# State space loop of a hybrid trunk step: one of the four products that turn the states forth goes by a ScalarE copy and Pool, and three inputs are scaled in front of the loop

## The chip, the cores and the metric

The kernel runs on one core of a Trainium2 chip. The metric is device time of one execution in microseconds (us). The engines are TensorE (PE in the rows; PEld is its weight load), VectorE (DVE), ScalarE (ACT), GpSimd (POOL, "Pool" in the text) and SyncE (SP), which issues most of the transfers.

## The reference, cut to what matters

Two layers run over a prompt group of 512 tokens and a sample group of 8 x 4 = 32 tokens with shared weights. Layer 1's token mixer is a diagonal complex state space:

```python
def _s5(u, h0_re, h0_im, a_re, a_im, log_dt, b_re, b_im, c_re, c_im, d_skip, w_glu):
    ...                                                  # ab = discretised pole, bb = discretised input matrix
    def block_step(carry, u_blk):
        h_re, h_im = carry
        bu_re = jnp.einsum('bcgi,gpi->bcgp', u_blk, bb_re)
        bu_im = jnp.einsum('bcgi,gpi->bcgp', u_blk, bb_im)
        bu_re = bu_re.at[:, 0].add(ab_re * h_re - ab_im * h_im)
        bu_im = bu_im.at[:, 0].add(ab_re * h_im + ab_im * h_re)
        ...
        _, _, s_re, s_im = lax.associative_scan(_cplx_affine_combine, (a_r, a_i, bu_re, bu_im), axis=1)
        y = (jnp.einsum('bcgp,gip->bcgi', s_re, c_re)
             - jnp.einsum('bcgp,gip->bcgi', s_im, c_im) + d * u_blk)
        return (s_re[:, -1], s_im[:, -1]), y
    ...
    z = jnp.einsum('bld,de->ble', jax.nn.gelu(y), w_glu)
    out = z[..., :D_MODEL] * jax.nn.sigmoid(z[..., D_MODEL:])
```

Each layer then adds a cross-attention to a memory of 256 rows, whose keys and values are `mem @ w_k` and `mem @ w_v`, and a squared-ReLU MLP.

## The kernel before, in words

Prompt and sample go together: the activations are eight tiles of 128 channels x 544 columns, and in the state space layer the 544 columns are four groups of 136 (8 of the sample, 128 of the prompt). A weight block is used in two parts, high and low: ScalarE copies the high part (helper line L137, tile `whl`), and DVE or Pool subtracts it to get the low part (L177). For the eight memory key blocks of layer 1 it is Pool that subtracts.

The order of the work is written out by hand: `s5_layer` (L1811) appends steps to a list, and `run` calls them one after the other. Every engine executes its instructions in the order in which the steps emit them; the framework adds only the semaphore waits between engines. It adds them for PSUM by bank: two engines that touch the same bank wait for each other, also where the columns differ and where both only read.

The part that matters is the loop over the eight channel tiles, `kt` = 0 to 7. Its order on all engines is: states(0), K0; then for kt = 0 to 6: states(kt+1), from kt = 3 on parts(kt-3), the key block K(kt+1), outs(kt), from kt = 1 on fetch(kt-1). After it come four value blocks (L467), outs(7) and the gated product (L227, L215). In the texts below, E(m), K(m), outs(m) and so on stand for these steps' parts with index m.

- **states(m)** (L1918): TensorE multiplies the inputs into PSUM banks 0 to 3 (L1926, E(m), 16 instructions). ScalarE fills the decay factors `rho`. DVE turns the inputs back by a table `ro` of cosines and sines (L1937 twice, L1938, L1939, L1940, and L1942 for the sample), scans real and imaginary part in banks 4 and 5 (L1944 twice, tiles `ks`), and turns the states forth by four products of 128x512, two of each `ks` with the two halves of `ro` (L1954, L1955, for x = 1, then for x = 0). Pool adds and subtracts the products (L1956 for the outputs' states, L1957 for the last states); ScalarE copies the sample's start states in (`h0v`, two small copies). SP loads the tables of step m+2, and Pool scales the input of step m+2 (`scale`, L1907).
- **K(m)** (L450, 24 matmuls): one block of the memory keys of layer 1, put into bank 7, columns 0 to 255. ScalarE reads it out (`kv_out` L430: a copy of 128x256), and SP stores it.
- **outs(m)** (L1967): TensorE makes the output in four groups q = 0 to 3, each one L1975 and two L1978 (2 and 4 instructions in the trace). Groups 0 to 2 go to bank 6, group 3 to bank 7, columns 256 to 391. ScalarE applies gelu (128x408 and 128x136), and its queue stores the result.
- **parts(m)** (L1995): ScalarE copies the high part of a gelu output (128x544), Pool subtracts for the low part (L2000).

In front of the loop, `begin` (L1887) makes the scale row `ru`; DVE scales the inputs 0 and 1, and Pool sets the first columns of the two `rho` tiles (L1903).

Of the kernel before, what the change touches and what calls it, by code (L numbers as in the profile page):

```python
# [9 lines left out]
AF = mybir.ActivationFunctionType  # L10
# [7 lines left out]
KT = 8  # L18
# [39 lines left out]
class Trunk:  # L58
# [1752 lines left out]
    def s5_layer(self, att_begin, kre):  # L1811
        nc, I, O = self.nc, self.I, self.O
        V = nc.vector
# [6 lines left out]
        def tr(kt):  # L1820

            if kt % 3 == 2:
                return [t[:, :512] for t in D["r2"]]
            return [D["ar"][0][:, 2048 + kt % 3 * 1024 + x * 512 :][:, :512] for x in range(2)]

        def load_e(kt):
            if kt < KT:
                nc.sync.dma_start(te(kt), self.tab[kt][:, 0:1024])

        def load_r(kt):  # L1830
            if kt < KT:
                for x, r in enumerate(tr(kt)):
                    nc.sync.dma_start(r, self.tab[kt][:, 2560 + 512 * x : 3072 + 512 * x])
# [53 lines left out]
        def begin():  # L1887

            y, b0, b1 = self.sm["y"], self.aux[1], self.aux[0][:, 128:256]
            for j in range(4):  # L1890
                nc.tensor.transpose(b0[:, j * 128 : j * 128 + 128], y[:, j : j + 1].to_broadcast([P, 128]), self.ident)
            nc.tensor.transpose(b1, y[:, 4:5].to_broadcast([P, 128]), self.ident)
            D["ru"] = ru = self.rb[:, :TAU]
            for s in range(4):
                a, r = 3 - s, slice(32 * s, 32 * s + 32)
                self.act(ru[r, 8:], b0[r, a * 128 : a * 128 + 128], AF.Copy)
                V.tensor_copy(ru[r, :8].rearrange("p (f j) -> p f j", f=2),
                              b1[r].rearrange("p (j x) -> p j x", x=32)[:, :, a : a + 8 : 4].rearrange("p j f -> p f j"))
            scale(0)
            scale(1)  # L1900
            D["rho"] = [self.slot(), self.slot()]
            for t in D["rho"]:
                nc.gpsimd.memset(q4(t)[:, :, :1], 0.0)  # L1903

        def scale(kt):
            up = D["up"][kt].rearrange("p (q j) -> p q j", q=4)
            (nc.gpsimd if kt > 1 else V).tensor_mul(up, up, D["ru"].unsqueeze(1).to_broadcast([P, 4, TAU]))  # L1907
# [6 lines left out]
        ks = [self.banks[:, 4 + x] for x in range(2)]  # L1914
# [3 lines left out]
        def states(kt):  # L1918
            def fn():
                E = te(kt)  # L1920
                up = D["up"][kt]
                for v in self.mmv:
                    self.touch(self.mm, v)
                for x in range(2):
                    for q in range(4):
                        nc.tensor.matmul(es[:, x, q // 2, q % 2], E[:, x * 512 + q * 128 : x * 512 + q * 128 + 128],  # L1926
                                         up[:, q * TAU : q * TAU + TAU], start=True, stop=True)
                ro = tr(kt)
                ah = D["ah"]
                qs = slice(4 * kt, 4 * kt + 4)  # L1930

                rho = D["rho"][kt % 2]
                self.act(q4(rho)[:, :, 1:], self.rho[:, qs].unsqueeze(2).to_broadcast([P, 4, 127]), AF.Copy)

                m = [self.slot()[:, :512] for _ in range(2)]
                for x in range(2):
                    V.tensor_mul(q22(m[x]), ec[:, x], q22(ro[1]))  # L1937
                V.tensor_mul(ec, ec, q22(ro[0]).unsqueeze(1).to_broadcast([P, 2, 2, 2, 128]))  # L1938
                V.tensor_add(q22(ks[0]), ec[:, 0], q22(m[1]))  # L1939
                V.tensor_sub(q22(ks[1]), ec[:, 1], q22(m[0]))  # L1940
                av = ah[:, :, qs].rearrange("p x (a q) j -> p x a q j", a=2)
                V.tensor_add(av, av, es[:, :, :, :, :8])  # L1942
                for k in ks:
                    V.tensor_tensor_scan(k, rho[:, :512], k, 0.0, ALU.mult, ALU.add)  # L1944
                hh = [self.slot(), self.slot()]
                hv = [t.rearrange("p (q j) -> p q j", q=4) for t in hh]
                for x in range(2):
                    self.act(hv[x][:, :, :8], D["h0v"][:, x, qs], AF.Copy)
                    nc.gpsimd.memset(hv[x][:, :, 8:9], 0.0)
                hp = D["hp"]  # L1950

                for x, op in ((1, ALU.add), (0, ALU.subtract)):
                    p, r = self.slot(), self.slot()
                    V.tensor_mul(p[:, :512], ks[0], ro[x])  # L1954
                    V.tensor_mul(r[:, :512], ks[1], ro[1 - x])  # L1955
                    nc.gpsimd.tensor_tensor(hv[x][:, :, 9:], q4(p)[:, :, :127], q4(r)[:, :, :127], op=op)  # L1956
                    nc.gpsimd.tensor_tensor(hp[x][:, qs], q4(p)[:, :, 127], q4(r)[:, :, 127], op=op)  # L1957
                D["H", kt] = hh
                if kt == 0:
                    D["r2"] = [self.slot(), self.slot()]  # L1960
                load_e(kt + 2)
                load_r(kt + 2)
                if kt + 2 < KT:
                    scale(kt + 2)
            return Step(fn, deep=1)

        def outs(kt):  # L1967
# [83 lines left out]
        def last_kv():  # L2051
# [3 lines left out]

        kv[0][1].deep = -1
        S += [Step(aux_kv), kv[0].popleft(), Step(stats, deep=-1), kv[0].popleft(), Step(self.stat_rsqrt, deep=-1), Step(begin),
              kv[0].popleft(), kv[0].popleft(), Step(free_kv), states(0), kv[1].popleft()]
        for kt in range(KT - 1):
# [161 lines left out]
```

## Time and profile before

| what | value |
|---|---|
| median of 3 runs | 1545.75 us (1545.52 to 1546.58) |
| the profiled execution, its own time | 1544.09 us |
| span of the profiled execution | 1542.3 us |
| mean granted TensorE clock | 0.991 |
| busy share of the span | PE 97%, DVE 66%, ACT 45%, POOL 13% |
| the state space loop | about 833 to 899 us of the span |

The profile is of one execution, which took 1544.09 us by its own time; the span of its instructions is 1542.3 us, and the 1.8 us between them lie around the instructions. Busy shares over the whole span are means over stages with different limits, so the loop is read by itself: by windows of 10 us, by the timeline of each engine, and by the chain of waits.

### The profile page before, as it was taken

To read this page: it belongs to the slowest core of one execution; us is meant where nothing else is said; L and a number is where in the kernel's file an instruction comes from. 1 tells how busy PE (TensorE), PEld (TensorE's weight loads), DVE (VectorE), ACT (ScalarE), POOL (GpSimd) and SP (SyncE) were. 2 spreads that over 40 slices of the span, in tenths; PEclk is the share of its full clock that TensorE was granted. 3 is DMA by queue.
4 is the path that set the end of the run, shared out by engine and by line. 5 is a ranking of instruction groups with operands and counts; after the bars stand their busy time and mean duration, and the time that the engine had idled before them with its cause. 6 is when DMAs were issued, how large, how long until landed. Compare 5 with 4: busy or idle time off the path is not lost.

```text
span 1542.3 us, 29330 instructions
## 1 busy us (share of the span) xinstructions
PE 1494.1 (97%) x11927; PEld 1446.7 (94%) x11927; DVE 1015.5 (66%) x2068; ACT 687.2 (45%) x1278; POOL 200.3 (13%) x167
## 2 busy tenths in 40 slices
PE   8999979999999999999999999999999999999996
PEld 8999869988999999999998889998899999999995
DVE  6896786444577566666756964553479677585864
ACT  6332454343445433665444443343357445272543
POOL 2555550000000000000103760000000000000001
PEclk9999989999999999999999999999999999999998
DMA  7765526363323343333587975336322414141211
GB/s 278 182 153 148 169 85 230 131 242 124 111 80 105 135 134 134 134 134 107 179 268 230 333 242 184 110 137 264 133 69 83 137 55 149 44 139 53 85 53 59
DMA packets 92535, 224.49 MB, mean 146 GB/s; under 512 B 12496, under 2 KB 42976, under 8 KB 88304
## 3 DMA queue, kind: packets, MB, share of 16 engines
q1 hardware_dynamic: 87440, 211.06, 40.3%
q0 software_dynamic: 1792, 6.37, 2.3%
q10 hardware_dynamic: 3168, 5.18, 0.9%
q8 instruction: 94, 1.54, 0.4%
q14 instruction: 41, 0.34, 0.1%
HBM read 192.78 MB, written 29.80 MB: 144 GB/s over the span
## 4 chain that ended last, share of the span: by engine, by line
PE 78%; DVE 8%; ACT 1%; issue 1%; POOL 1%; DMA 0%; SPq 0%; ACTq 0%; DVEq 0%; POOLq 0%
PE banks L215 44%; PE banks L1403 12%; PE banks L1295 10%; PE banks L467 2%; PE banks L956 2%; PE banks L892 2%; PE banks L973 1%; PE banks L876 1%; PE banks L227 1%; PE banks L1382 1%; DVE banks L1944 1%; ACT slot L137 1%; DVE banks L702 1%; PE banks L1766 0%; DVE whl L177 0%
## 5 line engine op out<-in xcount | busy, mean ns | idle before, releaser
L215 PE MATMUL banks<-slot,whl 128*128 128x272 f32 x6264 | 802.1, 289 | 5.8 <-ACT slot L137 2.4
L215 PEld LDWEIGHTS banks<-slot,whl 128*128 128x128 f32 x6264 | 791.1, 188 | 11.0 <-ACT slot L137 4.5
L137 ACT ACTIVATE whl<-wst 128x1024 fp32r<-128x1024 f32 (+1 forms) x236 | 218.7, 930 | 134.8 <-PE banks L1403 47.8
L177 DVE TENSOR_TENSOR whl<-wst,whl 128x1024 fp32r<-128x1024 f32 x137 | 171.1, 1252 | 92.1 <-ACT whl L137 89.4
L137 ACT ACTIVATE slot<-banks 128x512 fp32r<-128x512 f32 (+8 forms) x134 | 61.1, 479 | 144.1 <-PE banks L215 42.2
L1403 PE MATMUL banks<-slot,whl 128*128 128x272 f32 x912 | 120.2, 289 | 0.5 <-DVE rt L1316 0.5
L1403 PEld LDWEIGHTS banks<-slot,whl 128*128 128x128 f32 x912 | 116.7, 188 | 0.7 <-DVE rt L1316 0.7
L1295 PE MATMUL banks<-slot,whl 128*128 128x272 f32 x756 | 97.2, 288 | 0.9 <-DVE tmp L1413 0.9
L1295 PEld LDWEIGHTS banks<-slot,whl 128*128 128x128 f32 x756 | 95.6, 188 | 1.1 <-ACT whl L137 1.1
L1525 POOL TENSOR_TENSOR slot<-slot,slot 128x272 f32<-128x272 f32 x6 | 5.0, 855 | 616.1 <-ACT slot L137 616.1
L137 ACT ACTIVATE slot<-x,vec 128x544 fp32r<-128x544 f32 (+2 forms) x50 | 35.3, 728 | 108.7 <-DVE x L2013 43.8
L1413 DVE TENSOR_TENSOR tmp<-banks,rb 128x544 f32<-128x544 f32 x30 | 21.7, 725 | 83.0 <-PE banks L1403 83.0
L1403 PE MATMUL banks<-slot,arena_mlp 128*128 128x272 f32 x528 | 71.5, 288 | 0.4 <-DVE rt L1316 0.4
L702 DVE SCALAR_TENSOR_TENSOR banks<-slot,vec,banks 128x512 f32<-128x512 f32 x90 | 67.9, 755 | 2.8
L1403 PEld LDWEIGHTS banks<-slot,arena_mlp 128*128 128x128 f32 x528 | 68.2, 188 | 0.6 <-DVE rt L1316 0.6
L1295 PE MATMUL banks<-slot,arena_mlp 128*128 128x272 f32 x504 | 65.3, 288 | 0.4 <-DVE acc L1330 0.4
L1295 PEld LDWEIGHTS banks<-slot,arena_mlp 128*128 128x128 f32 x504 | 63.9, 188 | 0.7 <-DVE acc L1330 0.6
L425 POOL TENSOR_TENSOR slot<-slot,slot 128x512 fp32r<-128x512 f32 x4 | 6.1, 1566 | 371.4 <-ACT slot L137 371.4
L137 ACT ACTIVATE tmp<-x 128x544 f32<-128x544 f32 x40 | 25.9, 647 | 63.4 <-DVE x L1099 39.7
L137 ACT ACTIVATE tmp<-banks 128x544 f32<-128x544 f32 x32 | 19.9, 623 | 76.5 <-PE banks L215 76.5
L177 POOL TENSOR_TENSOR whl<-wst,whl 128x1024 fp32r<-128x1024 f32 x19 | 45.3, 2386 | 57.4 <-ACT whl L137 57.4
L250 DVE TENSOR_TENSOR slot<-tmp,slot 128x544 fp32r<-128x544 f32 x32 | 23.2, 726 | 41.5 <-ACT slot L137 41.5
(280 smaller groups left out, 2063.3 us busy)
## 6 DMA issues: line engine op xcount, KB each, us to landing
wst<-in_w SPq DMA_DIRECT2D x231, 512.0 KB, 4.4
arena_att<-in_kc SPq DMA_DIRECT2D x16, 1024.0 KB, 5.0
arena_att<-in_vc SPq DMA_DIRECT2D x16, 1024.0 KB, 5.3
tab<-arena_prep SPq DMA_DIRECT2D x24, 512.0 KB, 3.8
whl<-in_w POOLq DMA_DIRECT2D x12, 512.0 KB, 6.0
arena_s<-tab SPq DMA_DIRECT2D x8, 768.0 KB, 5.5
arena_s<-tab SPq DMA_DIRECT2D x8, 512.0 KB, 6.3
arena_s<-tab SPq DMA_DIRECT2D x12, 256.0 KB, 5.2
```

Source lines behind the costliest of these rows:

```text
L137: self.nc.scalar.activation(out, in_, func, **kw)
L177: eng.tensor_sub(t[:, 1].bitcast(F32R), src, t[:, 0])
L215: self.nc.tensor.matmul(ps[:, c, :HALF], w, x[:, c * HALF : c * HALF + HALF], start=first and n == 0, stop=last and n == len(seq) - 1)
L227: self.nc.tensor.matmul(ps[:, c, :HALF], self.w8(b, kt)[wi], rhs[kt][xi].bitcast(F32R)[:, c * HALF : c * HALF + HALF], start=first and kt ...
L250: self.nc.vector.tensor_sub(l.bitcast(F32R), src_h if src_l is None else src_l, h)
L467: nc.tensor.matmul(ps[m], self.memt(2 * kp + k2, xi)[:, m * 128 : m * 128 + 128], t[:, wi, k2 * 512 : k2 * 512 + 512], start=kp == 0 and k ...
L702: nc.vector.scalar_tensor_tensor(A, win(k), w(k), A, op0=ALU.mult, op1=ALU.add)
L892: nc.tensor.matmul(o, qs[qi], ks[ki], start=e == 0 and i == 0, stop=e == 1 and i == 2)
L956: nc.tensor.matmul(ps[e], vs[vi], xs[xi], start=m == 0 and i == 0, stop=m == 1 and i == 2)
L1295: nc.tensor.matmul(bank, u[:, wi, k * 128 : k * 128 + 128], x[k][xi].bitcast(F32R), start=n == k == 0, stop=n == 2 and k == 3)
L1403: nc.tensor.matmul(ps[:, c, :HALF], us[kt // 4][:, wi, kt % 4 * 128 : kt % 4 * 128 + 128], M["h"][kt][xi].bitcast(F32R)[:, c * HALF : c * ...
L1413: job("V", 0.7, lambda: V.tensor_mul(self.c2(t), self.psv(ps), self.c2(self.rb)), [*bk, "rb"], [("t", o % 2)])
```

## The change

In `begin`, the inputs 0 to 4 are scaled, and not 0 and 1 alone; `scale` still puts 0 and 1 on DVE and the others on Pool. In the loop, only states(3), (4) and (5) scale an input (5, 6 and 7). In states(m), ScalarE copies `ks[1]` (the scan in bank 5) to a slot `kc`, Pool multiplies that with `ro[1]`, and the subtraction for x = 0 takes this product; DVE keeps three products.

```diff
-            scale(0)
-            scale(1)
+            for kt in range(5):
+                scale(kt)
...
+                kc, r1 = self.slot(), self.slot()
+                self.act(kc[:, :512], ks[1], AF.Copy)
+                nc.gpsimd.tensor_mul(r1[:, :512], kc[:, :512], ro[1])
+
                 for x, op in ((1, ALU.add), (0, ALU.subtract)):
-                    p, r = self.slot(), self.slot()
+                    p, r = self.slot(), r1
                     V.tensor_mul(p[:, :512], ks[0], ro[x])
-                    V.tensor_mul(r[:, :512], ks[1], ro[1 - x])
+                    if x:
+                        r = self.slot()
+                        V.tensor_mul(r[:, :512], ks[1], ro[0])
                     nc.gpsimd.tensor_tensor(hv[x][:, :, 9:], q4(p)[:, :, :127], q4(r)[:, :, :127], op=op)
                     nc.gpsimd.tensor_tensor(hp[x][:, qs], q4(p)[:, :, 127], q4(r)[:, :, 127], op=op)
...
-                if kt + 2 < KT:
+                if 2 < kt < KT - 2:
                     scale(kt + 2)
```

In the changed file the Pool product is L1954, the products on DVE are L1958 and L1961, the sums on Pool L1962 and L1963, and the matmuls of outs L1981 and L1984.

The order of ScalarE around states(1), K1 and outs(0), before and after. `slot_8969` and `slot_8974` take K1 out of bank 7; the 128x408 and 128x136 rows are the gelus of outs(0).

```order
L137 ACTIVATE slot_8789<-rho 128x4x127
L137 ACTIVATE slot_8923<-slot_8472 128x4x8
L137 ACTIVATE slot_8924<-slot_8472 128x4x8
L137 ACTIVATE slot_8969<-banks 128x256 [waits PE_49]
L137 ACT_TABLE_LOAD [waits DVE_49]
L137 ACTIVATE slot_8984<-banks 128x408 [waits PE_49]
L137 ACTIVATE slot_8984<-banks 128x136 [waits PE_49]
```

```order
L137 ACTIVATE slot_8792<-rho 128x4x127
L137 ACTIVATE slot_8927<-slot_8472 128x4x8
L137 ACTIVATE slot_8928<-slot_8472 128x4x8
L137 ACTIVATE slot_8933<-banks 128x512 [waits DVE_49]
L137 ACTIVATE slot_8974<-banks 128x256 [waits PE_49]
L137 ACT_TABLE_LOAD
L137 ACTIVATE slot_8989<-banks 128x408 [waits PE_49]
L137 ACTIVATE slot_8989<-banks 128x136 [waits PE_49]
```

The new copy `kc` of states(1), which waits for DVE (the scan), now stands ahead of the copy that takes K1 out.

The order of TensorE in the changed kernel from group 2 of outs(0) on to K2. The L1981 row with a wait is the first of group q = 3; in the order before, its L1975 has the same wait at the same place.

```order
L1981 MATMUL banks<-slot_8197,arena_s_8350 128x136
L1984 MATMUL banks<-slot_8853,arena_s_8350 128x136
L1984 MATMUL banks<-slot_8854,arena_s_8350 128x136
L1981 MATMUL banks<-slot_8197,arena_s_8350 128x136 [waits Activation_49]
L1984 MATMUL banks<-slot_8853,arena_s_8350 128x136
L1984 MATMUL banks<-slot_8854,arena_s_8350 128x136
L1926 MATMUL banks<-slot_8475,arena_s_8349 128x136 [waits DMAHW2_49,DMAHW1_49,DMAHW7_49,DMAHW0_49,DVE_49]
L1926 MATMUL banks<-slot_8475,arena_s_8349 128x136 x7
L450 MATMUL banks<-slot_7902,whl_81 128x256 [waits Activation_49]
```

Nothing moved on TensorE; group 3 waits for ScalarE, and E(2) (L1926) stands behind it. The wait is for the ScalarE instruction that takes K1 out of the bank.

The order of DVE at the end of states(1) in the changed kernel:

```order
L1944 SCALAR_TENSOR_TENSOR banks<-slot_8792,banks 128x512 [waits DVE_49]
L1958 TENSOR_TENSOR slot_8937<-banks,arena_s_8349 128x512 [waits DVE_49]
L1961 TENSOR_TENSOR slot_8939<-banks,arena_s_8349 128x512 [waits Activation_49]
L1958 TENSOR_TENSOR slot_8943<-banks,arena_s_8349 128x512
L1937 TENSOR_TENSOR slot_9006<-banks,slot_8874 128x512 [waits DMAHW4_49,PE_49]
```

One product of four has gone, and L1961, which reads the same bank as the new copy, waits for ScalarE.

## Rows read from the trace of the kernel before

**Rows 1.** The page: busy time of each engine, and the engines' shares of the chain that ended last.

```profile
PE 1494.1 (97%) x11927; PEld 1446.7 (94%) x11927; DVE 1015.5 (66%) x2068; ACT 687.2 (45%) x1278; POOL 200.3 (13%) x167
PE 78%; DVE 8%; ACT 1%; issue 1%; POOL 1%; DMA 0%; SPq 0%; ACTq 0%; DVEq 0%; POOLq 0%
```

**Rows 2.** A window of 10 us in the loop: stretch and its length, busy time (and instructions) of PE, PEld, DVE, ACT and POOL, then granted clock, DMA share and GB/s.

```profile
863.00:873.00 10.00, 9.18 (x79) 8.98 (x78) 9.90 (x15) 3.54 (x8) 7.99 (x10) 1.00 1.03 356
```

**Rows 3.** The timeline of DVE: start, duration, then line, operation and tiles, and in brackets the idle time before with what ended it. From the scans of states(0) to the first product of states(1), and the scans of states(7).

```profile
839.12 2.33 DVE L1944 TENSOR_TENSOR_SCAN banks<-slot,banks 128x512 f32<-128x512 f32 x2
841.37 0.67 DVE L1954 TENSOR_TENSOR slot<-banks,arena_s 128x512 f32<-128x512 f32 x1
...
843.75 1.28 DVE L1937 TENSOR_TENSOR slot<-banks,arena_s 128x512 f32<-128x512 f32 x2
847.66 2.33 DVE L1944 TENSOR_TENSOR_SCAN banks<-slot,banks 128x512 f32<-128x512 f32 x2
849.90 0.67 DVE L1954 TENSOR_TENSOR slot<-banks,arena_s 128x512 f32<-128x512 f32 x1
...
898.87 2.33 DVE L1944 TENSOR_TENSOR_SCAN banks<-slot,banks 128x512 f32<-128x512 f32 x2
```

**Rows 4.** The timeline of ScalarE, same columns: the fill of `rho` and the small copies behind it, and the copy that takes K(4) out of bank 7; then a copy of 128x544 by the rows of one shape between 833 and 911 us (operation, shape, count, busy time, mean ns of one, idle time before).

```profile
867.03 0.61 ACT L137 ACTIVATE slot<-rho 128x508 f32<-128x508 f32 x1
867.55 0.88 ACT L137 ACTIVATE slot<-slot 128x32 f32<-128x32 f32 x3
870.08 0.38 ACT L137 ACTIVATE slot<-banks 128x256 f32<-128x256 f32 x1 [1.66 <-POOL sm L1957]
...
L137 ACT ACTIVATE slot<-slot 128x544 fp32r<-128x544 f32 x5 | 3.2, 643 | 0.0
```

**Rows 5.** The timeline of Pool, same columns: the weight parts in front of the loop and the first sum of states(0); then a step from the first sum of states(4) to that of states(5), with the scale of an input and the subtraction of a part in it.

```profile
830.16 4.81 POOL L177 TENSOR_TENSOR whl<-wst,whl 128x1024 fp32r<-128x1024 f32 x2 [20.00 <-ACT whl L137]
835.47 2.40 POOL L177 TENSOR_TENSOR whl<-wst,whl 128x1024 fp32r<-128x1024 f32 x1 [0.49 <-ACT whl L137]
842.71 1.28 POOL L1956 TENSOR_TENSOR slot<-slot,slot 128x508 f32<-128x508 f32 x1 [4.76 <-DVE slot L1955]
...
876.85 1.29 POOL L1956 TENSOR_TENSOR slot<-slot,slot 128x508 f32<-128x508 f32 x1 [2.00 <-DVE slot L1955]
...
879.63 1.35 POOL L1907 TENSOR_TENSOR slot<-slot,rb 128x544 f32<-128x544 f32 x1
880.92 1.35 POOL L2000 TENSOR_TENSOR slot<-slot,slot 128x544 fp32r<-128x544 f32 x1
...
885.39 1.29 POOL L1956 TENSOR_TENSOR slot<-slot,slot 128x508 f32<-128x508 f32 x1 [0.70 <-DVE slot L1955]
```

**Rows 6.** The timeline of TensorE: E(1); K(5); and from group 0 of outs(6) the L1978, after idle time.

```profile
839.26 2.12 PE L1926 MATMUL banks<-slot,arena_s 128*128 128x136 f32 x16 [0.73 <-DVE slot L1942]
875.47 3.08 PE L450 MATMUL banks<-slot,whl 128*128 128x256 f32 x24
...
896.65 0.73 PE L1978 MATMUL banks<-slot,arena_s 128*128 128x136 f32 x4 [0.80 <-POOL slot L1956]
```

**Rows 7.** The chain of waits, in order of time (start, length, what): outs(4) from group 0, which had waited for Pool, then group 1, group 3 and E(6); and the value blocks, which follow group 3 of outs(6) at the end of the loop.

```profile
879.58 0.73 PE banks L1978 x4
880.31 0.23 PE banks L1975 x2
880.54 0.46 PE banks L1978 x4
...
881.70 0.23 PE banks L1975 x2
881.93 0.46 PE banks L1978 x4
882.40 1.87 PE banks L1926 x16
...
899.47 11.20 PE banks L467 x48
```

**Rows 8.** Two hand-overs. ScalarE starts a copy when DVE has ended L1099; TensorE loads the second half of E(0), which waits for ScalarE's two copies of 128x512 out of PSUM (833.36, followed on ScalarE by the row at 834.33). Timelines of DVE, ScalarE and TensorE's weight load.

```profile
819.80 0.73 DVE L1099 TENSOR_TENSOR x<-x,tmp 128x544 f32<-128x544 f32 x1
820.62 0.66 ACT L137 ACTIVATE tmp<-x 128x544 f32<-128x544 f32 x1 [6.51 <-DVE x L1099]
833.36 1.09 ACT L137 ACTIVATE slot<-banks 128x512 f32<-128x512 f32 x2 [1.50 <-PE banks L467]
834.33 1.06 ACT L137 ACTIVATE whl<-wst 128x1024 fp32r<-128x1024 f32 x1
834.50 0.99 PEld L1926 LDWEIGHTS banks<-slot,arena_s 128*128 128x128 f32 x8 [0.22 <-ACT slot L137]
```

**Rows 9.** Idle time of TensorE and the granted clock behind it, elsewhere in the span: rows of the timeline with the gap in brackets, the windows before and after the first (columns as in rows 2), and the key block right behind the second.

```profile
204.00:206.00 2.00, 0.40 (x3) 0.40 (x4) 1.44 (x2) 0.42 (x3) 0.00 (x0) 1.00 0.00 0
205.60 0.38 PE L287 MATMUL banks<-ones,slot 128*128 128x2 f32 x2 [2.80 <-DVE slot L735]
206.00:208.00 2.00, 2.00 (x9) 1.76 (x10) 0.00 (x0) 1.98 (x2) 1.04 (x1) 0.57 0.06 12
28.25 0.62 PE L287 MATMUL banks<-ones,slot 128*128 128x2 f32 x4 [1.57 <-ACT slot L137]
28.73 4.62 PE L450 MATMUL banks<-arena_mem,whl 128*128 128x256 f32 x24
```

## The prediction

> **What bounds the kernel now.** I read the page first: TensorE is busy 97% of the span and carries 78% of the chain that ended last, DVE 8% and Pool 1% [rows 1]. Such shares are means over stages, so next comes a window inside the loop. There it is otherwise: in 10 us DVE is busy 9.90 us, TensorE 9.18, Pool 7.99 and ScalarE 3.54, at granted clock 1.00, the upper of its two levels, 2.4 GHz [rows 2]. So in this stage DVE has no room, and a product fewer on it could be worth something. The timeline of DVE gives the pace: the scan pairs of step 0 and step 7 start at 839.12 and 898.87, 8.54 us a step [rows 3].
>
> Then one has to see who runs how far ahead, for that decides what the change holds up. ScalarE runs a step ahead of DVE: it takes K(4) out of bank 7 at 870.08 [rows 4], while the scans of step 4 (839.12 and four paces) only end at 875.6. TensorE waits about 0.8 us a step for Pool, ahead of the first state product of outs [rows 5, 6], and for nothing else between.
>
> I write s(m) for the end of the scans of step m: s(0) = 839.12 + 2.33 = 841.45, s(7) = 901.20 [rows 3]. Before, the last group of outs(6) hands over to the value blocks at 899.47 [rows 7], 1.73 us ahead of s(7).
>
> **The change, part by part.**
>
> *Scales in front.* Three of Pool's 1.35 us [rows 5] come ahead of its weight parts, 4.0 us in all. Those parts end at 837.9; K(0) needs the low half a little after, and behind K(0) TensorE has 0.73 us to spare before E(1) [rows 6]; the first sum on Pool is at 842.71 after 4.76 us of idle time [rows 5]. The part that K(0) needs comes first among them, so I cost this edit at nothing. If that cover is gone, it is the delay of one part less the 0.73 us, at most 3.3 us, once.
>
> *The product leaves DVE.* Four products take 843.75 - 841.37 = 2.38 us, 0.60 each [rows 3]. The price on DVE is that L1961 waits for the copy, which reads the same bank. The copy starts 0.09 us after the scan, as the hand-over from DVE to ScalarE shows (820.62 after 820.53), and lasts 0.485 to the next instruction of ScalarE (two in 834.33 - 833.36) [rows 8]; L1961 could start at 0.52 after the scan (0.60 less the 0.08 by which the product's record overlaps the scan's), and the copy, 0.605 when its end is counted (1.09 - 0.485), ends at 0.69: about 0.16 later. So the first interval, in which TensorE is still ahead, gets 0.60 - 0.16 = 0.44 shorter: s(1) = 849.99 - 0.44 = 849.55.
>
> *Pool.* A product from slots has no row; its bounds are the nearest Pool rows, 1.28 for 128x508 and 1.35 for 128x544 [rows 5], and I take 1.28. The fullest step of Pool (scale and part in it) takes 885.39 - 0.70 - 876.85 = 7.84 [rows 5], with the product 9.1. The sums end about 0.7 + 1.28 + 2.78 (876.85 to 879.63) = 4.8 us after s(m).
>
> *The copy on ScalarE.* This is the term that decides. The copy waits for the scan of step m, and ScalarE's queue is in order. In the order of ScalarE the read-out of K(m) stands right behind it, from step 4 on with the copy of parts(m-4) between. Before, that read-out was done 5.5 us ahead of the scan's end; now it cannot start until after it. Who waits for it: group 3 of outs(m-1) writes the same bank 7, and the order of TensorE shows its wait for ScalarE. Behind group 3 on TensorE is E(m+1), without which DVE cannot begin step m+1. So a circle closes that was open: scan(m), copy, read-out, group 3, E(m+1), DVE, scan(m+1). One turn:
>
> - scan to the end of copy and read-out: 0.09 + 0.485 [rows 8] + 0.38 [rows 4] = 0.955;
> - to TensorE: 0.05, as the load at 834.50 follows the copies' end at 834.45 [rows 8];
> - group 3: 0.23 + 0.46 in stride, and the 0.27 that group 0 shows more after a wait (0.73 for 0.46) [rows 7], taken as 0.23 since the first instruction of the two waits here: 0.92;
> - E(m+1): 1.87 [rows 7], and 0.05 to DVE, taken as the other hand-over;
> - from the second L1937, which needs the second half of E, to the end of the scans: 849.99 - 843.75 - 0.60 [rows 3] = 5.64.
>
> That is 9.49 us a step, for m = 1, 2, 3. For m = 4, 5, 6 the copy of parts comes in: 0.64 [rows 4] less 0.10, the overlap of neighbours that 867.03 + 0.61 against 867.55 shows [rows 4]: 10.03 us. Pool's step is full (9.1) only where the turn is 10.03, and 7.8 or less before (no part to subtract), so Pool does not set the pace. DVE then has about 1.5 us of idle time a step and its saving is worth nothing there.
>
> *The sum.* s(1) = 849.55; three times 9.49: s(4) = 878.02; three times 10.03: s(7) = 908.11. Behind it once more copy, parts, read-out, hand-over and group 3 of outs(6): 0.575 + 0.54 + 0.38 + 0.05 + 0.92 = 2.47, that is 910.58 against 899.47: **11.1 us later**. By parts: -0.44, +2.9 and +4.5 in the intervals, and +4.2 because the last group comes 2.47 after s(7) and no longer 1.73 ahead of it. After that TensorE has the value blocks, 11.20 us [rows 7], which cover the sums of step 7 (4.8 us), and runs on as before; I see nothing that gives time back. The profiled execution took 1544.09, so it would be 1555.2; its own time is 1.66 under the median of the runs, and against the median I say **1556.9 us**.
>
> *Bounds.* Below: the restart costs nothing (-0.23) and the read-out overlaps like its neighbours (-0.10), over six turns and the end -2.3: 1554.6. Above: E takes the 2.12 that it takes after idle time [rows 6] and the copy 0.61 in place of 0.485, +0.37 a turn: 1559.5.
>
> That the wait in group 3 lasts is in no row of before, for there the read-out came early; only the order shows it. The Trainium skill's page "PSUM — Partial Sum Buffer", section "PSUM bank collisions raise a hardware error", says that engines have to be kept apart by bank (and partition quadrant) and not by address, so columns 0 to 255 and 256 to 391 of one bank do not pass each other. By that rule the sum above holds; if addresses counted, it would be the first rival's.
>
> **The rivals.**
>
> *The hold is harmless, DVE's saving counts (1544).* That needs a read-out of K(m) that is not late, or a group 3 that does not wait for it. Then a step is 8.54 - 0.60 = 7.94, six intervals to s(6) give -3.6, and Pool, whose sums end 0.8 later, takes that back: -2.8, or 1543.0. Where Pool's 9.1 a step is over 7.94, in two steps, it lags by 2.3: -0.5, or 1545.2. Against it speak the orders of ScalarE and of TensorE; for it, that the loop is DVE's by [rows 2]. It decides from the point where the read-out comes later than 1 us behind s(m). 7%. It is the case that is not slower, and it lies within 0.2% (3.1 us, about what can be told from no change here) or just at its edge.
>
> *The clock falls (1561 to 1569).* The circle leaves TensorE idle between group 2 and group 3. After E (at 3.85 us of a turn) come K 3.08 [rows 6] and three groups of 0.69 [rows 7], which end at 9.0; group 3 follows 1.0 us into the next turn, or 1.55: 1.5 us idle for m = 1 to 3 and 2.6 later. Elsewhere a gap of 2.80 was followed by a clock of 0.57, that is mostly the lower level of 1.2 GHz, and one of 1.57 by a key block of 4.62 us in place of 3.08 [rows 6, 9]; but before the first of these TensorE had been nearly idle for longer (0.40 of 2 us) [rows 9], which in the loop it is not. A fall that meets group 3 and E costs up to 0.69 + 1.87 = 2.6 a turn; in two to five turns +5 to +13; a fall that only meets K is hidden by the gap. 14%. The Trainium skill's page "TensorE: Matmul & The Clock Gate", section "HAM oscillation — how this bites in real kernels", tells of a loop whose waits throttle TensorE again in every pass; that would be the upper end here.
>
> *Transfers late (1560 or more).* SP's store of K(m) now waits for the late read-out, and the table loads behind it with it, some 5 us. The steps are longer too and the DMA share of 1.03 [rows 2] is relieved, so I give it 3%.
>
> **How the numbers follow.** Forecast 76% (1554.6 to 1559.5), harmless 7%, clock 14%, transfers 3%. The range 1553 to 1563 takes in the forecast with its bounds and the small end of clock and transfers, and leaves out some 17%. Faster by over 0.2%: 2%; within: 6%, both from the harmless case with its Pool lag; slower: 92%.
>
> **What would show it.** Right: scan pairs 9.5 us apart at first and 10.0 from step 4 on; the copies of 128x256 on ScalarE right behind those of 128x512, and those behind a scan; L1981 of group 3 after 1.5 to 2.6 us of idle time put down to ScalarE; DVE idle ahead of L1937, put down to TensorE; value blocks some 11 us later, and the same gap to the end. Wrong: scan pairs 8 us apart, Pool busy through, a clock under 1.00 between 850 and 910, or a wait on a transfer ahead of E or outs.

## The result, and the profile after

The changed kernel takes 1560.41 us in the median of 4 runs (1558.21 to 1561.39), the kernel before 1545.63 on the same chip (4 runs, 1544.76 to 1546.58): **1.0101 times the time, 95% interval 1.0089 to 1.0113**, 14.8 us slower by the medians. (The ratio is an estimate of its own; the quotient of the two medians, 1.0096, lies in its interval.) The forecast was 1556.9 with a range of 1553 to 1563. The profiled execution took 1558.21 us by its own time, 14.1 more than the profiled one of before. One execution of experiment 4 below, of 1829.19 us at a mean granted clock of 0.75, is left out of that experiment's numbers.

The page of the changed kernel, same rows as [rows 1]: busy times hardly moved, and ScalarE and transfers now show in the chain.

```profile
PE 1500.0 (96%) x11927; PEld 1451.7 (93%) x11927; DVE 1009.8 (65%) x2060; ACT 690.4 (44%) x1286; POOL 209.5 (13%) x175
PE 77%; DVE 7%; ACT 2%; DMA 2%; issue 1%; SPq 1%; DVEq 0%; ACTq 0%
```

The timeline of DVE in the changed kernel, the eight scan pairs of the loop, which answer to [rows 3]; the two L1937 of step 3 stand behind the scans of step 2, and the second L1937 of step 7 behind those of step 6 (columns: start, duration, line, operation and tiles; in brackets the idle time before and what ended it).

```profile
838.34 2.33 DVE L1944 TENSOR_TENSOR_SCAN banks<-slot,banks 128x512 f32<-128x512 f32 x2
846.46 2.33 DVE L1944 TENSOR_TENSOR_SCAN banks<-slot,banks 128x512 f32<-128x512 f32 x2
857.60 2.33 DVE L1944 TENSOR_TENSOR_SCAN banks<-slot,banks 128x512 f32<-128x512 f32 x2
...
862.82 0.69 DVE L1937 TENSOR_TENSOR slot<-banks,arena_s 128x512 f32<-128x512 f32 x1 [0.86 <-PE banks L1926]
863.75 0.69 DVE L1937 TENSOR_TENSOR slot<-banks,arena_s 128x512 f32<-128x512 f32 x1 [0.23 <-PE banks L1926]
...
867.07 2.33 DVE L1944 TENSOR_TENSOR_SCAN banks<-slot,banks 128x512 f32<-128x512 f32 x2
876.60 2.33 DVE L1944 TENSOR_TENSOR_SCAN banks<-slot,banks 128x512 f32<-128x512 f32 x2
888.41 2.33 DVE L1944 TENSOR_TENSOR_SCAN banks<-slot,banks 128x512 f32<-128x512 f32 x2
898.43 2.33 DVE L1944 TENSOR_TENSOR_SCAN banks<-slot,banks 128x512 f32<-128x512 f32 x2
...
905.17 0.69 DVE L1937 TENSOR_TENSOR slot<-banks,arena_s 128x512 f32<-128x512 f32 x1 [0.18 <-PE banks L1926]
...
908.50 2.33 DVE L1944 TENSOR_TENSOR_SCAN banks<-slot,banks 128x512 f32<-128x512 f32 x2
```

The intervals are 8.12, 11.14, 9.47, 9.53, 11.81, 10.02 and 10.07 us, before 8.54 each. Four of the six turns are at the forecast 9.49 and 10.03; two, the first and the fourth, take 1.7 and 1.8 us more.

One undisturbed turn, m = 6: the scans end at 900.76. The timeline of ScalarE (copy of the scan, copy of parts(2), read-out of K(6) with the gelu of groups 0 to 2):

```profile
900.85 0.60 ACT L137 ACTIVATE slot<-banks 128x512 f32<-128x512 f32 x1 [5.08 <-DVE banks L1944]
901.35 0.65 ACT L137 ACTIVATE slot<-slot 128x544 fp32r<-128x544 f32 x1
901.89 0.78 ACT L137 ACTIVATE slot<-banks 128x256 f32<-128x256 f32 x2
```

The timeline of TensorE in the changed kernel: the turn m = 1 with group 3 (L1981, L1984) and E(2), then m = 2, then m = 6, and the value blocks.

```profile
849.75 0.53 PE L1981 MATMUL banks<-slot,arena_s 128*128 128x136 f32 x2 [2.26 <-ACT slot L137]
850.09 1.10 PE L1984 MATMUL banks<-slot,arena_s 128*128 128x136 f32 x4
850.98 3.25 PE L1926 MATMUL banks<-slot,arena_s 128*128 128x136 f32 x16
...
860.89 0.50 PE L1981 MATMUL banks<-slot,arena_s 128*128 128x136 f32 x2 [1.74 <-ACT slot L137]
861.23 0.63 PE L1984 MATMUL banks<-slot,arena_s 128*128 128x136 f32 x4
861.69 2.02 PE L1926 MATMUL banks<-slot,arena_s 128*128 128x136 f32 x16
...
880.50 0.56 PE L1981 MATMUL banks<-slot,arena_s 128*128 128x136 f32 x2 [2.33 <-ACT slot L137]
...
902.32 0.50 PE L1981 MATMUL banks<-slot,arena_s 128*128 128x136 f32 x2 [2.34 <-ACT slot L137]
902.66 0.63 PE L1984 MATMUL banks<-slot,arena_s 128*128 128x136 f32 x4
903.12 2.02 PE L1926 MATMUL banks<-slot,arena_s 128*128 128x136 f32 x16
...
913.05 11.44 PE L467 MATMUL banks<-whl,slot 128*128 128x512 f32 x48
```

Here is the whole circle in rows. ScalarE has stood idle for 5.08 us when the scan ends, then copies, does the parts, and takes K(6) out; TensorE, idle for 2.34 us, is released by ScalarE at 902.32, does group 3 and E(7), and DVE's second L1937 starts at 905.17, 4.41 us after the scans' end (forecast 3.84 + 0.54). One sign is less clean than forecast: for m = 5 and 6 the profile puts the idle time ahead of the first L1937 (1.46 and 1.53 us) down to Pool, but that is not on the path: the second L1937, on which the sum rests, is released by TensorE there too and starts 2.05 us after E at m = 6, as it does at m = 2 (2.06). In the turn m = 1 the same instructions of TensorE take 1.10 for 0.63 and 3.25 for 2.02: the clock. The windows of the changed kernel (columns as in [rows 2]):

```profile
843.00:853.00 10.00, 7.34 (x48) 6.94 (x47) 7.59 (x11) 3.96 (x9) 8.37 (x11) 0.85 0.58 184
863.00:873.00 10.00, 8.21 (x72) 8.01 (x70) 8.62 (x12) 3.85 (x9) 6.98 (x11) 1.00 1.00 313
873.00:883.00 10.00, 7.67 (x57) 7.47 (x56) 7.50 (x11) 3.34 (x10) 8.27 (x10) 0.89 0.91 297
903.00:913.00 10.00, 7.72 (x66) 7.52 (x65) 8.15 (x11) 3.91 (x9) 7.78 (x10) 1.00 0.69 200
```

The granted clock was 1.00 through this loop before, in every window of 10 us from 833 to 913; now it is 0.85 and 0.89 in the two windows with the long turns. DVE went from 9.90 us busy in ten to 7.5 to 8.6. The value blocks start 72.38 us after the first scans' end (913.05 - 840.67), before 57.77 (899.22 - 841.45, the row below): the 14.6 us are all in the loop.

```profile
899.22 11.45 PE L467 MATMUL banks<-whl,slot 128*128 128x512 f32 x48
```

### The profile page after: what moved, and what is told of

Its sections match the earlier page's. It is cut to its first block, busy times and chain, and to the rows that moved or that the text cites. A ratio compares the mean times of both kernels' runs of the same rounds, so it can differ in the third digit from the quotient of the medians.

```text
span 1556.4 us, 29332 instructions
## 1 busy us (share of the span) xinstructions
PE 1500.0 (96%) x11927; PEld 1451.7 (93%) x11927; DVE 1009.8 (65%) x2060; ACT 690.4 (44%) x1286; POOL 209.5 (13%) x175
## 4 chain that ended last, share of the span: by engine, by line
PE 77%; DVE 7%; ACT 2%; DMA 2%; issue 1%; SPq 1%; DVEq 0%; ACTq 0%
PE banks L215 44%; PE banks L1403 12%; PE banks L1295 10%; PE banks L467 2%; PE banks L892 2%; PE banks L956 2%; PE banks L973 1%; PE banks L876 1%; ACT slot L137 1%; DMA wst<-in_w 1%; PE banks L227 1%; PE banks L1382 1%; DMA arena_s<-tab 1%; DVE banks L1944 1%; PE banks L1926 1%
## 5 line engine op out<-in xcount | busy, mean ns | idle before, releaser
L137 ACT ACTIVATE slot<-banks 128x512 fp32r<-128x512 f32 (+9 forms) x142 | 64.7, 486 | 155.5 <-DVE banks L1944 43.5
```

The costliest lines, as they stand in the source:

```text
L137: self.nc.scalar.activation(out, in_, func, **kw)
```

## The experiments

Each ratio is against the kernel before, run on the same chip beside it, with its 95% interval.

**1. The copy behind the read-out of K(m).** `states` is cut in two ahead of the new copy, and the second half emitted behind K(m); the loads of step m+2 and the scale stand in that half and move along, and K0 and states(0) are treated alike:

```diff
-            S.append(states(kt + 1))
+            first, late = states(kt + 1)
+            S += [first, kv[1].popleft(), late]
             if kt >= 3:
                 S.append(parts(kt - 3))
-            S.append(kv[1].popleft())
             S.append(outs(kt))
```

> The changed kernel with one move: the ScalarE copy of the scan, and with it the products and Pool's work of the step, stand behind the read-out of K(m) in the order. ScalarE still copies, Pool still multiplies, DVE still keeps three products. Theory of the hold (the copy, waiting for the scan, held the read-out, group 3 and the next E behind it): the circle is open, scan pairs come about 8.1 us apart as the one interval of the changed kernel that had no hold showed (838.34 to 846.46, 8.12), TensorE has no wait of 1.7 to 2.3 us ahead of group 3, the clock stays at 1.00, and the time is 1544 to 1547, near the kernel before and some 14 under the changed one. Rival (the added work itself costs: Pool's product of 1.28 in each step, or a copy on ScalarE that gets in the way of DVE): nothing of that is taken away here, so it stays within 3 us of 1560.

1545.22 us (12 runs), **1.0002 (0.9993 to 1.0012)**. Scan pairs 8.11 to 8.19 us apart, clock 1.00. One move in the order takes the whole loss away; all the added work is still there. But the 0.36 us a step that DVE gained did not arrive either. TensorE in this kernel, group 0 of outs(6) and the value blocks (the view ends at 905 us, so the last row holds 25 of the 48):

```profile
896.58 0.73 PE L1990 MATMUL banks<-slot,arena_s 128*128 128x136 f32 x4 [1.25 <-POOL slot L1968]
...
899.14 6.07 PE L467 MATMUL banks<-whl,slot 128*128 128x512 f32 x25
```

and Pool, the added product in steps 5 and 6, 9.05 us apart with no idle time between:

```profile
883.56 1.30 POOL L1960 TENSOR_TENSOR slot<-slot,slot 128x512 f32<-128x512 f32 x1
...
892.61 1.29 POOL L1960 TENSOR_TENSOR slot<-slot,arena_s 128x512 f32<-128x512 f32 x1
```

Pool's full steps (product, scale and part) are longer than DVE's and set the end: the value blocks start 57.9 us after s(0), before 57.8.

**2. Group 3 behind E.** The other arc cut: E(m+1) goes ahead of group 3 on TensorE, ScalarE's order stays.

```diff
-            S.append(outs(kt))
+            S.append(outs(kt, range(3)))
+            if kt + 2 < KT:
+                S.append(inputs(kt + 2))
+            S.append(outs(kt, range(3, 4)))
```

(`inputs` holds the matmuls L1926 of `states`.)

> The changed kernel with another arc of the circle cut: on TensorE the matmuls E(m+1) are issued ahead of group 3 of outs(m-1). ScalarE's order is untouched, so the read-out of K(m) is still held until the scan of step m has ended. Theory of the hold through TensorE: group 3 still starts 1.0 to 1.5 us after each scan's end, but DVE no longer waits for E, the scan pairs come 8.1 to 8.5 us apart, TensorE is idle for less than 1 us a step and the clock stays at 1.00; group 3 of outs(6) still comes about 2.5 us after the last scan, so 1546 to 1550. If instead the late read-out costs by something else than E behind group 3 (the store of K and the table loads behind it on SP, the gelu and what follows on ScalarE), the scan pairs stay 9.5 to 10 us apart and the time within 3 us of 1560.

1547.53 us (11 runs), **1.0019 (1.0009 to 1.0028)**, scan pairs 8.11 to 8.19 apart. TensorE: group 3 of outs(5) now follows E(7) without a gap, K(7) waits 0.37 us for ScalarE, and only the last group 3, which has no E ahead of it, still waits:

```profile
893.23 0.50 PE L1985 MATMUL banks<-slot,arena_s 128*128 128x136 f32 x2
893.57 0.63 PE L1988 MATMUL banks<-slot,arena_s 128*128 128x136 f32 x4
894.57 3.12 PE L450 MATMUL banks<-slot,whl 128*128 128x256 f32 x24 [0.37 <-ACT slot L137]
...
901.34 0.50 PE L1985 MATMUL banks<-slot,arena_s 128*128 128x136 f32 x2 [1.09 <-ACT slot L137]
...
902.06 11.44 PE L467 MATMUL banks<-whl,slot 128*128 128x512 f32 x48
```

So the late read-out costs through E behind group 3: the stores and loads of SP, which stand behind the same late read-out here, cost nothing that shows. The end piece is what is left in the loop: the value blocks start 59.3 us after s(0), 1.6 later than before. The median is 2.9 us over that of before; the cause of the other 1.3 us is not shown.

**3. The gap filled.** Group 2 of outs is computed again, with the same result:

```diff
-                for q in range(4):
+                for q in (0, 1, *[2] * (1 if kt == 7 else 4 if kt == 0 or kt > 2 else 3), 3):
```

> The changed kernel with work added: group 2 of outs is computed again, three times in outs(0) and outs(3) to outs(6) and twice in outs(1) and outs(2), with the same result, 0.69 us each, so that TensorE's idle time ahead of group 3 falls from 1.7 to 2.3 us to some 0.3 us. Nothing of the circle is changed. If idle time in the circle is what makes the clock fall (two of six turns in the profile after, 3.4 us over the sum without falls), there are no falls, every turn takes 9.5 and then 10.05 us, and the time is 1556 to 1558, less than the changed kernel's 1560.4 although TensorE does 12.4 us more of work. If the falls have another cause, they stay: 1558 to 1562. If group 3 does not wait for the read-out but for TensorE's own work, the added work is on the path and it gets slower, 1565 and more.

1557.14 us (5 runs, 1556.17 to 1557.49), **1.0075 (1.0061 to 1.0088)**: 3.3 us under the changed kernel's median, and under every run of the copy alone on the same chip (experiment 4), with 13.1 us more of work on TensorE. (The 12.4 of the expectation is a miscount: five times three and twice two are 19 repeats of 0.69 us, and the page has 114 more matmul instructions, six for each.) The idle time ahead of group 3 is 0.17 and 0.34 us in the first two turns, the granted clock is 1.00 in every window of 10 us from 833 to 913, and the scan pairs are 9.47 to 9.53 and 10.01 to 10.13 us apart in every turn. TensorE and the window of the turn m = 1:

```profile
850.02 0.50 PE L1981 MATMUL banks<-slot,arena_s 128*128 128x136 f32 x2 [0.17 <-ACT slot L137]
850.36 0.63 PE L1984 MATMUL banks<-slot,arena_s 128*128 128x136 f32 x4
850.82 2.02 PE L1926 MATMUL banks<-slot,arena_s 128*128 128x136 f32 x16
```

```profile
843.00:853.00 10.00, 9.42 (x78) 9.02 (x78) 8.68 (x13) 3.96 (x9) 8.37 (x11) 1.00 0.62 198
```

Without the idle time there are no falls, and without them the kernel is where the sum put it.

**4. The copy alone**, on the kernel before; and the same kernel once more for a profile.

```diff
+                kc = self.slot()
+                self.act(kc[:, :512], ks[1], AF.Copy)
+
                 for x, op in ((1, ALU.add), (0, ALU.subtract)):
```

> The kernel before with nothing but the ScalarE copy of the scan added, at the place in the order that the change gives it, into a slot that nobody reads: four products on DVE, no product on Pool, the scales where they were. Theory of the hold: the circle is the same as in the changed kernel, 9.5 and 10.05 us a turn, and DVE's fourth product is hidden in its wait for E except in the first interval (0.6 longer); so 1557 to 1562, and as many falls of the clock. If the changed kernel's saving on DVE is worth something inside its turns, this is slower by up to 7 x 0.6 = 4.2 us more: 1564. If Pool's product or the scales in front are what costs, it stays near 1546.

1561.24 us (3 runs, 1558.40 to 1562.11), **1.0099 (1.0080 to 1.0118)**: a copy that nobody reads costs as much as the whole change.

> The kernel with the ScalarE copy alone once more, for its profile: scan pairs 9.5 us apart for m = 1 to 3 and 10.05 for m = 4 to 6 where the clock does not fall, 1.6 to 1.8 more where it does; four products on DVE, and DVE still idle ahead of L1937 (by about 0.6 us less than in the changed kernel), which waits for E. If DVE's fourth product were on the path, the scan pairs would be 10.1 and 10.6 us apart.

1560.85 us (one run). DVE in it, steps 2 and 3:

```profile
858.74 2.33 DVE L1944 TENSOR_TENSOR_SCAN banks<-slot,banks 128x512 f32<-128x512 f32 x2
...
863.95 0.69 DVE L1937 TENSOR_TENSOR slot<-banks,arena_s 128x512 f32<-128x512 f32 x1 [0.34 <-PE banks L1926]
864.88 0.69 DVE L1937 TENSOR_TENSOR slot<-banks,arena_s 128x512 f32<-128x512 f32 x1 [0.24 <-PE banks L1926]
...
868.21 2.33 DVE L1944 TENSOR_TENSOR_SCAN banks<-slot,banks 128x512 f32<-128x512 f32 x2
```

The intervals are 8.71, 10.89, 9.47, 9.53, 11.59, 10.02 and 10.07 us: with four products on DVE the turns are as long as with three, the fourth lies in DVE's wait for E (0.34 here, 0.86 ahead of the same L1937 in the changed kernel), and the clock falls in the same two turns (0.88 in the window 843 to 853, 0.92 and 0.91 in 873 to 893). The falls cost 1.4 and 1.6 us there, a little less than expected.

**5. The scales alone** (the first and the last piece of the change's diff, on the kernel before).

> The kernel before with the scales alone moved: the inputs 0 to 4 in front of the loop, 5 to 7 in states(3) to (5), nothing else. Theory: Pool's three scales in front lie under the weight parts' slack, and in the loop Pool was not the bound; so within 1 us of the kernel before (by the profile after, TensorE began E(1) with the same slack of some 0.5 us). Rival (K(0) waits for its low weights, which Pool now makes 4 us later): up to 3 us slower.

1544.09 us (12 runs), **0.9998 (0.9989 to 1.0007)**, scan pairs 8.53 apart as before. Costed at nothing, and it is.

**6. Read-out first, scales early.** Experiment 1, and `if kt < 3: scale(kt + 5)` in place of `if 2 < kt < KT - 2: scale(kt + 2)`.

> The version with the copy behind the read-out of K(m), and now the inputs 5, 6 and 7 scaled in states(0), (1) and (2) in place of (3), (4) and (5), so that no step of Pool has both a scale and the subtraction of a part. In the first version DVE ran at 8.17 us a step, 0.36 under the kernel before, and gave it back at the end, where group 0 of outs(6) waited 1.25 us for Pool, whose full steps took 9.05 us. If that lag of Pool's is where the saving went, it goes: Pool's steps are 7.8 us at most, outs(6) ends 56.5 to 57 us after the first scans' end (before 58.0), so 1.0 to 1.5 us faster than before. If the saving is lost to something else (the product's 1.25 us on Pool ahead of the sums), no change, within 0.5 us.

1543.52 us (11 runs), **0.9990 (0.9982 to 0.9999)**. The value blocks start 56.4 us after s(0), 1.4 nearer than before, Pool's steps are spread out, and group 0 of outs(6) no longer waits for Pool. So that is where DVE's saving had gone in experiment 1. TensorE's value blocks (s(0) is at 840.55):

```profile
896.95 11.44 PE L467 MATMUL banks<-whl,slot 128*128 128x512 f32 x48
```

**7. The copy behind the gelus.** The second half of `states` behind `outs(kt)`, DVE's two products of `ks[0]` ahead of that of `ks[1]`, scales as in 6.

```diff
+            S += [first, kv[1].popleft(), outs(kt), late]
...
+                p1, p0, r0 = [self.slot() for _ in range(3)]
+                V.tensor_mul(p1[:, :512], ks[0], ro[1])
+                V.tensor_mul(p0[:, :512], ks[0], ro[0])
+                V.tensor_mul(r0[:, :512], ks[1], ro[0])
```

> All three holds taken out: the copy stands behind the gelus of outs(m-1) in ScalarE's order (so neither the read-out of K(m) nor the gelus wait for the scan), DVE takes its two products of the first scan ahead of the one that reads the copied bank (so it does not wait for ScalarE), and the inputs 5 to 7 are scaled in states(0) to (2). DVE's step is then 8.54 - 0.60 = 7.94 us, Pool's 7.8 at most, TensorE's 7.7 with some 0.3 us of wait for Pool. outs(6) ends 6 x 7.94 + 7.45 = 55.1 us after the first scans' end, before 58.0: 2 to 3 us faster than the kernel before (0.13 to 0.2%). Rival: TensorE or the transfers (DMA share 1.03 before) cannot follow at 7.94, the scan pairs stay at 8.1 to 8.2, and it is 1 to 1.5 us faster, like the version without these two moves, or not faster at all.

1546.19 us (12 runs), **1.0017 (1.0004 to 1.0030)**: a miss. The first two intervals were 7.94, the next two 8.17 and 8.47, and then E(5), E(6) and E(7) on TensorE waited 1.04, 0.76 and 2.58 us for their tables; E(7):

```profile
894.80 2.09 PE L1928 MATMUL banks<-slot,arena_s 128*128 128x136 f32 x16 [2.58 <-DMA arena_s<-tab]
```

The second half of `states` also issues the loads for step m+2, and by the move they came behind the load of outs on SP. I had not followed them.

**8. The same, with those loads back in the first half.**

> The version with the copy behind the gelus, and the loads of E's and the turning tables for step m+2 issued again in the first half of the step, ahead of SP's store of K(m). In the version without this the scan pairs came 7.94 us apart for two steps, and then E(5), E(6) and E(7) waited 1.04, 0.76 and 2.58 us for their table, because the loads stood behind the store and behind the load that waits for outs. If that queue was the cause, these waits go, the scan pairs come 7.95 to 8.1 us apart, and outs(6) ends about 55.2 us after the first scans' end (57.8 before, by the same rows): 2 to 3 us faster than the kernel before. If the transfers as a whole cannot follow a step of 7.94 (2.97 MB a step, DMA share 1.03 to 1.06), E still waits and it stays within 1.5 us of the kernel before.

1543.79 us (11 runs), **0.9995 (0.9986 to 1.0004)**. The waits for tables are gone, but the intervals are 7.93 twice and then 8.14 to 8.30. DVE and TensorE:

```profile
891.13 0.69 DVE L1969 TENSOR_TENSOR slot<-banks,arena_s 128x512 f32<-128x512 f32 x1 [0.27 <-ACT slot L137]
```

```profile
895.16 0.73 PE L1989 MATMUL banks<-slot,arena_s 128*128 128x136 f32 x4 [0.54 <-POOL slot L1971]
```

By these rows a new circle: the gelus of outs(m-1) hold the copy of step m, Pool's product and sums follow it, outs(m) waits for Pool, and its gelus hold the next copy. That is read from the waits and was not tested by itself.

**9. Read-out first, scales early, two products of the first scan first** (6 with the product order of 7), run twice.

> The version with the read-out first and the scales early, in which DVE takes its two products of the first scan ahead of the one of the copied bank. The wait of 0.22 us a step for ScalarE's copy goes: 8.17 to 7.95 us a step, six steps 1.3 us, outs(6) ends 55.1 to 55.4 us after the first scans' end (56.4 without): 2.5 to 3 us faster than the kernel before, 1.0 to 1.5 faster than without this move. Rival: the loads stand where they stood and the DMA share was 1.05 already, so E or the products wait for a table, and nothing is gained over the version without, or up to 2 us lost.

1542.63 us (11 runs, 1539.85 to 1545.81), **0.9995 (0.9986 to 1.0004)**.

> The last version once more (read-out first, scales early, two products of the first scan first), to see whether its gain holds: its profile showed the 7.94 us a step that were expected and the end of outs(6) 2.5 us nearer, but its runs were spread from 1539.9 to 1545.8 and the interval of the ratio took in 1. By the loop alone 2.2 to 2.7 us under the kernel before, a ratio of 0.9983 to 0.9986; if the time outside the loop varies by as much, the interval takes in 1 again.

1544.18 us (12 runs), **0.9996 (0.9987 to 1.0004)**. The loop did what was expected in both profiles: intervals of 7.93 but for one of 8.18, the value blocks 55.3 us after s(0), 2.5 nearer than before. DVE in the first of them, steps 0 and 1, and TensorE's value blocks:

```profile
837.35 2.33 DVE L1946 TENSOR_TENSOR_SCAN banks<-slot,banks 128x512 f32<-128x512 f32 x2
845.28 2.33 DVE L1946 TENSOR_TENSOR_SCAN banks<-slot,banks 128x512 f32<-128x512 f32 x2
```

```profile
894.97 11.44 PE L467 MATMUL banks<-whl,slot 128*128 128x512 f32 x48
```

The time does not show it: the medians are 2.2 and 0.1 us under those of before, and both intervals take in 1. The time outside the loop varies by more than this from run to run (the first scans of the profiles here start between 837.35 and 841.04 us). Whether 9 is faster than 6 or than the kernel before stays open; only 6 has an interval under 1, and barely.

## Why the prediction was right

The mechanism was right; the number was right with some help. The sum's own bounds were 1554.6 to 1559.5, and the median of 1560.41 lies above them. It is in the range because the range also took in the small end of the clock rival, and that is what happened: one of the signs listed as wrong, a clock under 1.00 between 850 and 910, was there.

**The copy on ScalarE**, the term that decided, held at its joints. Experiments 1 and 2 cut the circle at two places, and the loss went, in experiment 2 all but 2.9 us of it; experiment 4 made the circle with nothing else, and the loss came. One turn was forecast at 9.49 and 10.03 us and measured at 9.47, 9.53, 10.02 and 10.07. The pieces were a little off both ways: group 3 starts 0.96 us after the scans' end at m = 2 (forecast 1.01), E 1.76 (1.93), and the second L1937 3.82 (3.84).

**The wait in group 3**, which only the order showed, is there: TensorE is released by ScalarE, although K(m) lies in columns 0 to 255 of the bank and group 3 in 256 to 391. The Trainium skill's page "PSUM — Partial Sum Buffer", section "PSUM bank collisions raise a hardware error", asks for a guard by bank and partition quadrant, whatever the address; the trace agrees (2.34 us of idle time ended by ScalarE at m = 6). The wait that the trace shows is the one that the framework adds; whether the hardware needs it, and what group 3 in another bank would give, was not tried.

**The product off DVE.** First interval 8.12 (forecast 8.10); L1961 starts 0.75 us after L1958 in place of 0.60. Inside the turns the saving was worth nothing, as experiment 4 shows with 9.47 and 9.53 for both.

**The scales and Pool**: nothing, by experiment 5. Pool's product takes 1.28 us, the value taken.

**What was mis-sized: the clock.** It was a rival at 14%, apart from the forecast, and it came on top of it: two of six turns, 1.65 and 1.78 us, together 3.4. The sum of 11.1 and this is 14.5, against 14.6 in the profile's loop. The step that failed is the argument against it, that TensorE had been nearly idle for longer before the first fall elsewhere [rows 9] and would not be in the loop. That was a wrong reading: the gap of 2.80 us ahead of 205.60 begins at 202.80, so the window 204 to 206 with its 0.40 us of work lies mostly in the gap itself. Ahead of the gap TensorE worked without a break, as this row of before shows:

```profile
201.39 1.41 PE L467 MATMUL banks<-whl,arena_mem 128*128 128x512 f32 x5
```

So the rows of before spoke for the rival and not against it. In the loop TensorE was busy for 7.34 and 7.67 of 10 us in the two windows with the falls, and the clock fell all the same. The price of a fall, up to 2.6 us a turn, was an upper end; the falls cost two thirds of it, because they did not cover all of group 3 and E: in the turn m = 1 the first row of group 3 takes 0.53 us for 0.50, and E 1.23 us more in place of 1.87.

The Trainium skill's page "TensorE: Matmul & The Clock Gate", section "HAM oscillation — how this bites in real kernels", tells of a loop that is throttled again in every pass. Here it was two passes of six, in both profiles the same two.

**Not settled:** why those two. Idle times of 2.26 (m = 1) and 2.33 us (m = 4) were followed by a fall, 1.74 and 1.78 were not, and neither were 2.34, 2.34 and 2.28 for m = 5, 6 and 7; so the gap alone doesn't tell it. The other runs of the changed kernel took up to 3.2 us more than the profiled one at mean clocks of 0.986 to 0.988 against 0.989, which would fit one or two more falls, but there is no trace of them.

**The first rival** (hold harmless, 1543.0 to 1545.2) was close to the price of a kernel that we did not have yet: experiment 1 is that kernel, 1.0002 times the time of before, with Pool's lag in its full steps just where the rival put it. Its step was 8.18 and not the rival's 7.94, because DVE's product of the copied bank waits for the copy in every step. The chances given for this rival do not add up: 7% in one place, 2 and 6% in the other.

## What to carry to other kernels

An instruction that waits holds everything behind it on its engine, so before adding one, list what stands behind it there and who waits for that. Here a 0.5 us copy on an engine that was 35% busy in the loop cost 15 us, because the read-out of a bank stood behind it and the slow engine's next input behind that; one place further down it cost nothing. And a saving on the bounding engine is worth only as much as the next engine has room: with the hold gone it went to Pool's longest steps, until a scale was moved out of them.

## What the runs showed of the hardware

- Work added in an engine's idle time made the kernel faster: 13.1 us of repeated matmuls on TensorE in the gaps, and 3.3 us less time by the medians. With them the granted clock in the loop was 1.00, its upper level of 2.4 GHz; without them it was 0.85 and 0.89 in two windows of 10 us.
- A product of 128x512 from slots on Pool took 1.27 to 1.30 us, the same as a sum of 128x508 (1.26 to 1.31), with the next instruction 1.24 us later.
- Two engines that read the same bank one after the other, by a wait that the framework adds: DVE's product came some 0.15 to 0.23 us a step later for ScalarE's copy, and taking two products of the other bank first removed it (8.17 to 7.93 us a step).
